# A transformer block's down projection, regrouped: two runs of 16 Strassen tiles for two of 12, its sums folded in by accumulating DMAs

## The chip, the core and the metric

The kernel runs on one core of a Trainium2 chip. The metric is the device time of one execution in microseconds (us); the runs shown are three, and one further execution was recorded with the hardware profiler.

## The reference, cut to what matters

One decoder layer on x of 512 tokens by 2048 features, all in fp32: a norm, a mixer (an mLSTM and a retention head group) and its output projection, then a SwiGLU feed-forward layer with 5632 hidden columns, and a last norm.

```python
def swiglu_ffn(h, w_gu, w_down):
    gate, up = jnp.split(h @ w_gu, 2, axis=-1)
    return (jax.nn.silu(gate) * up) @ w_down
...
        x = x + mixers[layer](rms_norm(x, mix_norms[layer]))
        x = x + swiglu_ffn(rms_norm(x, ffn_norms[layer]), *ffn_weights[layer])
    return rms_norm(x, final_norm)
```

The change lies in the last product, `@ w_down`: its 5632 input rows are 44 tiles of 128, each to be multiplied with 16 tiles of 128 output rows, for 512 tokens.

## The kernel before, in words

**Numbers.** Every fp32 operand is split into a rounded high part and the rest: ScalarE (ACT) casts the high part, VectorE (DVE) subtracts it (`split`, L80). A plain product is then three matmuls of 512 columns (`mm3`, L88 to L91). A Strassen product (`strassen`, L208 on) takes a pair of output tiles and pairs of input tiles, splits the tokens in halves of 256, and makes seven products instead of eight; in each, an input pair costs one matmul of 512 columns (L220) and one of 256 (L219 or L223). For this it needs combinations of the activations (`combinations`, L153: from each pair x seven blocks `cb`, three by the function `two` at L158 and L159, four more after the sums of L165 to L168), and of each weight: four blocks b11, b21, b12, b22 are loaded (L227), added up (L232) and split (L84, L85).

**The down projection, stage by stage.** The hidden tiles lie in DRAM (`hd`), the residual too (`resd`). 44 tiles are taken as 4 plain, 12 by Strassen, 4 plain, 12 by Strassen, 4 and 4 plain, and the last 4 in the tail, which is written apart (L963 on) because it feeds the last norm and the output. A plain stage (`plainly`) goes through eight steps q. Step q loads a pair x of hidden tiles for the Strassen stage that follows (L863; into the ring `e4` of four buffers) and makes its combinations, loads the running sum into `r` (L865) and a block of weights (L75), makes 48 matmuls, adds their two sums to `r` on DVE (L871) and stores it (L872). A Strassen stage goes through eight pairs of output tiles, and stores its results apart (L880). The block `down` loads the sums into SBUF (`res`, L900), adds the matmuls of the last plain stages (L143), the stored Strassen results (L928, L929), loads the weights of the tail (`keep`, L919), and the tail follows.

**What sets the order.** Each engine runs its instructions in one order, which a scheduler has set when the program is built, and each waits for semaphores. SP issues nearly all the DMAs, one after the other: one whose buffer isn't free holds up those behind it. Two rings matter here: `e4` (four buffers of 512 KB, for x and for the Strassen results, two for a pair of output tiles) and `r4`, which serves sums and weights alike.

## Time and profile before the change

| | |
|---|---|
| runs shown | 2264.6, 2265.9, 2263.87 us; median 2264.6 us |
| profiled execution | 2263.38 us, of which the span between its first and last instruction is 2261.3 us |
| busy: TensorE, VectorE, ScalarE, GpSimd | 99%, 87%, 52%, 1% of the span |
| from the first plain stage to the tail | 1791.25 to 2202.84 us |
| tail | 2202.84 to 2261.30 us |

The profiled execution is 1.2 us under the median. A stage of the down projection begins with the first matmul of its kind; so its length is the difference of two start times of TensorE's timeline. The busy share of an engine is a mean over the stretch that the row names.

### The profile page before, as it was taken

The page shows a single profiled execution, that of the slowest core. Times are in us where ns is not written, and L with a number is a line of the kernel's source. Part 1 is how long each engine was busy: PE and PEld are TensorE (multiplying, and loading weights), DVE is VectorE, ACT ScalarE, POOL GpSimd, SP SyncE. Part 2 cuts the span into 40 slices and gives each one's busy share as a digit, 9 for nine tenths or more (in the row PEclk, how much of TensorE's full clock was granted, in tenths as well). Part 3 has the DMA queues.
Part 4 walks back from the last instruction along what each step waited for, and adds up shares of the span by engine and source line. Part 5 has one row for each costly group of instructions (what it writes and reads, how often), then busy time and mean ns, then how long its engine had stood idle before and what let it go on. Part 6 is the DMA issues. An engine that isn't in the chain of part 4 may idle for free.

```text
span 2261.3 us, 31321 instructions
## 1 busy us (share of the span) xinstructions
PE 2246.0 (99%) x12158; PEld 1928.9 (85%) x12158; DVE 1976.1 (87%) x2441; ACT 1165.0 (52%) x1558; POOL 18.4 (1%) x33
## 2 busy tenths in 40 slices
PE   9999999999999999999999999999999999999998
PEld 7888888888887888888888888888888888888887
DVE  7898999989978876899998999999999899899686
ACT  7444454545567744555445445544544545545334
POOL 0000000000000000000000000000000000000000
PEclk9999999999999999999999999999999999999999
DMA  7444433443475424433333333333333664764772
GB/s 272 160 140 140 131 128 134 140 133 129 140 243 177 154 89 142 165 112 127 124 113 118 125 118 117 126 126 117 112 126 117 214 227 151 265 203 157 257 254 75
DMA packets 133379, 344.67 MB, mean 152 GB/s; under 512 B 12496, under 2 KB 50800, under 8 KB 133232
## 3 DMA queue, kind: packets, MB, share of 16 engines
q1 hardware_dynamic: 132656, 341.64, 45.2%
q8 instruction: 95, 1.56, 0.3%
q10 hardware_dynamic: 576, 1.05, 0.1%
q14 instruction: 52, 0.43, 0.1%
HBM read 289.15 MB, written 53.49 MB: 152 GB/s over the span
## 4 chain that ended last, share of the span: by engine, by line
PE 94%; DVE 2%; DMA 2%; issue 1%; ACT 1%; POOL 0%; SPq 0%; POOLq 0%; ACTq 0%; DVEq 0%
PE a L220 28%; PE c L220 14%; PE a L223 12%; PE b L220 7%; PE c L223 6%; PE mm L91 3%; PE mm L90 3%; PE mm L89 3%; PE b L223 3%; PE a L219 2%; PE num L651 1%; PE c L90 1%; PE c L91 1%; PE c L89 1%; PE c L219 1%
## 5 line engine op out<-in xcount | busy, mean ns | idle before, releaser
L220 PE MATMUL a<-cb,whi 128*128 128x512 f32 x2508 | 901.3, 398 | 0.0
L223 PE MATMUL a<-cb,wlo 128*128 128x256 f32 x2186 | 613.2, 281 | 0.0
L220 PEld LDWEIGHTS a<-cb,whi 128*128 128x128 f32 x2508 | 467.1, 188 | 85.2 <-issue 0.2
L85 DVE TENSOR_TENSOR wlo<-r,whi 128x1024 fp32r<-128x1024 f32 (+1 forms) x402 | 480.0, 1195 | 63.0 <-ACT whi L84 61.1
L84 ACT CAST whi<-r 128x1024 fp32r<-128x1024 f32 (+1 forms) x402 | 414.4, 1032 | 92.4 <-PE b L220 61.4
L220 PE MATMUL c<-cb,whi 128*128 128x512 f32 x1248 | 453.9, 397 | 0.2 <-ACT whi L84 0.2
L84 ACT CAST whi<-raw 128x1024 fp32r<-128x1024 f32 (+1 forms) x237 | 246.2, 1039 | 348.0 <-PE c L220 126.1
L223 PEld LDWEIGHTS a<-cb,wlo 128*128 128x128 f32 x2186 | 412.9, 189 | 14.6 <-issue 0.2
L85 DVE TENSOR_TENSOR wlo<-raw,whi 128x1024 fp32r<-128x1024 f32 (+1 forms) x237 | 285.1, 1204 | 35.4 <-ACT whi L84 34.6
L223 PE MATMUL c<-cb,wlo 128*128 128x256 f32 x1088 | 305.2, 281 | 0.0
L220 PEld LDWEIGHTS c<-cb,whi 128*128 128x128 f32 x1248 | 234.9, 188 | 42.8 <-ACT whi L84 0.6
L232 DVE TENSOR_TENSOR r<-r,r 128x1024 f32<-128x1024 f32 (+1 forms) x180 | 210.8, 1171 | 14.5 <-DMA r<-in_w_gu 11.9
L220 PE MATMUL b<-cb,whi 128*128 128x512 f32 x612 | 222.7, 398 | 0.4 <-ACT whi L84 0.4
L223 PEld LDWEIGHTS c<-cb,wlo 128*128 128x128 f32 x1088 | 205.5, 189 | 7.2
L223 PE MATMUL b<-cb,wlo 128*128 128x256 f32 x534 | 149.9, 281 | 0.8 <-DVE wlo L85 0.8
L220 PEld LDWEIGHTS b<-cb,whi 128*128 128x128 f32 x612 | 115.2, 188 | 21.6 <-ACT whi L84 0.8
L271 DVE TENSOR_TENSOR e<-e 128x512 f32<-128x512 f32 x176 | 120.7, 689 | 7.9 <-ACT e L268 5.9
L268 ACT COPY e<-a 128x512 f32<-128x512 f32 x88 | 51.8, 588 | 142.7 <-PE a L220 142.7
L256 ACT COPY e<-a 128x512 f32<-128x512 f32 x88 | 51.8, 588 | 139.3 <-PE a L220 138.1
L232 DVE TENSOR_TENSOR r<-raw,r 128x1024 f32<-128x1024 f32 (+1 forms) x88 | 103.4, 1174 | 15.5 <-DMA r<-in_w_gu 7.3
L223 PEld LDWEIGHTS b<-cb,wlo 128*128 128x128 f32 x534 | 100.9, 189 | 4.5 <-DVE wlo L85 1.1
L232 DVE TENSOR_TENSOR r<-r,raw 128x1024 f32<-128x1024 f32 (+1 forms) x84 | 98.8, 1177 | 4.1 <-DMA raw<-in_w_gu 2.6
(350 smaller groups left out, 3373.1 us busy)
## 6 DMA issues: line engine op xcount, KB each, us to landing
r<-in_w_gu SPq DMA_DIRECT2D x85, 512.0 KB, 4.2
raw<-in_w_gu SPq DMA_DIRECT2D x83, 512.0 KB, 3.2
r<-in_w_in SPq DMA_DIRECT2D x61, 512.0 KB, 4.1
raw<-in_w_in SPq DMA_DIRECT2D x59, 512.0 KB, 3.3
pd<-e SPq DMA_DIRECT2D x64, 256.0 KB, 2.3
raw<-in_w_out SPq DMA_DIRECT2D x32, 512.0 KB, 3.4
raw<-in_w_down SPq DMA_DIRECT2D x32, 512.0 KB, 4.6
r<-in_w_pairs SPq DMA_DIRECT2D x34, 384.0 KB, 4.1
```

The lines of the kernel that those rows point to most:

```text
L84: nc.scalar.copy(hi, raw)
L85: nc.vector.tensor_tensor(out=lo, in0=raw, in1=hi.bitcast(F32), op=ALU.subtract)
L89: nc.tensor.matmul(acc, wh, xh, start=first, stop=False)
L90: nc.tensor.matmul(acc, wh, xl, start=False, stop=False)
L91: nc.tensor.matmul(acc, wl, xh, start=False, stop=last)
L219: nc.tensor.matmul(*small, start=False, stop=False, skip_group_check=not first)
L220: nc.tensor.matmul(acc, wh[:, ks], cbs[k][:, c, :, :], start=(first and k == 0), stop=last, skip_group_check=not first)
L223: nc.tensor.matmul(*small, start=False, stop=False, skip_group_check=not first)
L232: nc.vector.tensor_add(t, x, y)
L256: nc.scalar.copy(two[:, 1], a)
L268: nc.scalar.copy(one[:, 0], a)
L271: nc.vector.tensor_add(x[:, :, 0, :], x[:, :, 0, :], x[:, :, 1, :])
```

## The change

The 44 tiles are taken as 4 plain, 16 by Strassen (tiles 4 to 19), 4 plain (20 to 23), 16 by Strassen (24 to 39), and 4 in the tail (40 to 43). So both Strassen stages take eight input pairs instead of six, their blocks of weights are 512 KB instead of 384 KB, and the two plain stages ahead of the tail go. A plain stage now loads no running sum: ACT copies its two sums out of PSUM (L869), and they are stored in `plain_sums` (L870). From there, and from the results of the Strassen stages in SBUF, DMAs that add to what their destination holds bring them into the residual in DRAM: those of L880 (DRAM to DRAM) and L847 (SBUF to DRAM), each 128 rows of 512, 64 in all, issued by GpSimd (POOL), which issued none before. The tail's weights are loaded at L890, its hidden tiles at L900, the residual at L915; the tail's own lines stand 22 lower than before (L962 was L984).

```diff
-        sums = [dram.tile([KT // 2, P, 2, T], F32, name="sum%d" % i) for i in range(4)]
-
-        def parts_of(g):
+
+        def add_to_residual(q, n, t):
+            nc.gpsimd.dma_start(out=resd[q][:, n, :].rearrange("p (h t) -> p h t", h=2), in_=t, accum_op=ALU.add)
+
+        plain_sums = [dram.tile([KT // 2, P, 2, T], F32, name="sum%d" % i) for i in range(2)]
+
+        def plainly(g, src, base, out):
             parts = []
             for i in range(4 * g, 4 * g + 4, 2):
                 raw, hi, lo = r4([P, 2, T]), r4([P, 2, T], F32R), r4([P, 2, T], F32R)
...
                 nc.scalar.copy(hi, raw)
                 nc.vector.tensor_tensor(out=lo, in0=raw, in1=hi.bitcast(F32), op=ALU.subtract)
                 parts += [(hi[:, e, :], lo[:, e, :]) for e in range(2)]
-            return parts
-
-        def plainly(g, src, out):
-            parts = parts_of(g)
-            _, cbs, combine = combinations(cbp, None, lambda q: None, n_pairs=6)
+            _, cbs, combine = combinations(cbp, None, lambda q: None, KT // 2)
             for q in range(KT // 2):
-                if q < 6:
-                    x = ep.tile([P, 2, T], F32, name="e4")
-                    nc.sync.dma_start(out=x, in_=hd[4 * g + 4 + q:4 * g + 11 + q:6].rearrange("j p t -> p j t"))
+                x = ep.tile([P, 2, T], F32, name="e4")
+                nc.sync.dma_start(out=x, in_=hd[base + q:base + q + 9:8].rearrange("j p t -> p j t"))
                 r = r4([P, 2, T])
-                nc.sync.dma_start(out=r, in_=src[q])
-                wh, wl = (w.rearrange("p (n k c) -> p n k c", n=2, k=4) for w in weight(w_down[g][q]))
+                wh, wl = (w.rearrange("p (n k c) -> p n k c", n=2, k=4) for w in weight(src[q]))
                 for n in range(2):
                     acc = psf.tile([P, T], F32, name="abc"[(2 * q + n) % 3])
                     for k in range(4):
                         mm3(acc, wh[:, n, k, :], wl[:, n, k, :], parts[k][0], parts[k][1], k == 0, k == 3)
-                    nc.vector.tensor_add(r[:, n, :], r[:, n, :], acc)
+                    nc.scalar.copy(r[:, n, :], acc)
                 nc.sync.dma_start(out=out[q], in_=r)
-                if q < 6:
-                    combine(q, x)
-            return cbs
-
-        def kept_sum(out):
+                combine(q, x)
+                if q > 0:
+                    combine.sums(q - 1)
+            return cbs, lambda: combine.sums(KT // 2 - 1)
+
+        def into_residual(q, plain):
             def done(one, two):
+                for i in range(q + (q > 0), min(q + 2, KT // 2)):
+                    for n in range(2):
+                        nc.gpsimd.dma_start(out=resd[i][:, n, :], in_=plain[i][:, n, :], accum_op=ALU.add)
                 for n, t in enumerate((one[:, :, 0, :], two[:, :, 0, :])):
-                    nc.sync.dma_start(out=out[:, n, :].rearrange("p (h t) -> p h t", h=2), in_=t)
+                    add_to_residual(q, n, t)
 
             return done
 
-        for i, src in enumerate((resd, sums[0])):
-            cbs = plainly(4 * i, src, sums[2 * i])
-
-            his, los = (cbp.tile([P, 3, WU], F32R, name="cb") for _ in range(2))
-            more = itertools.cycle([w for n in range(3) for w in (None, (his[:, n], los[:, n]))])
-            all_pairs([(w_pairs[i, q], kept_sum(sums[2 * i + 1][q])) for q in range(KT // 2)], cbs, ep, psf, {})
-            more = itertools.repeat(None)
-        parts = parts_of(8)
+        kept, parts = [], []
+
+        def keep(i, tile_of):
+            raw = wp.tile([P, WU], F32, name="raw")
+            nc.sync.dma_start(out=raw, in_=w_last[i])
+            kept.append(split(raw, tile_of(), tile_of()))
+
+        for i in range(2):
+            cbs, last_sums = plainly(5 * i, w_down[5 * i], 4 + 20 * i, plain_sums[i])
+            all_pairs([(w_pairs[i, q], into_residual(q, plain_sums[i])) for q in range(KT // 2)], cbs, ep, psf, {}, last_sums)
+
+        for i in range(FT - 4, FT, 2):
+            raw = wp.tile([P, WU], F32, name="raw")
+            raw = raw.rearrange("p (j t) -> p j t", j=2)
+            nc.sync.dma_start(out=raw, in_=hd[i:i + 2].rearrange("j p t -> p j t"))
+            for e in range(2):
+                both, src = r4([P, 2, 2, HT], F32R), raw[:, e, :].rearrange("p (x t) -> p x t", x=2)
+                nc.scalar.copy(both[:, :, 0, :], src)
+                nc.vector.tensor_tensor(out=both[:, :, 1, :], in0=src, in1=both[:, :, 0, :].bitcast(F32), op=ALU.subtract)
+                parts.append(both)
+        for i in range(3):
+            keep(i, lambda: r4([P, WU], F32R))
 
     with ExitStack() as down:
         dp = down.enter_context(tc.tile_pool(name="dp", bufs=2, reuse_waits="tile"))
         ep = down.enter_context(tc.tile_pool(name="ep2", bufs=4, side="right", reuse_waits="tile"))
         psd = down.enter_context(tc.tile_pool(name="psd", bufs=1, space=bass.MemoryType.PSUM, reuse_waits="tile"))
-        accs.append(psd)
         for q in range(KT // 2):
             pairs[q] = dp.tile([P, 2, T], F32, name="res", bufs=8)
-            nc.sync.dma_start(out=pairs[q], in_=sums[2][q])
-
-        def group(g):
-            raw = dp.tile([P, 4, T], F32, name="hr", bufs=1)
-            both = dp.tile([P, 4, 2, T], F32R, name="hs")
-            nc.sync.dma_start(out=raw, in_=hd[4 * g:4 * g + 4].rearrange("j p t -> p j t"))
-            if g < FT // 4 - 1:
-                src, hi, lo = raw, both[:, :, 0, :], both[:, :, 1, :]
-            else:
-                both = both.rearrange("p j x (h t) -> p j x h t", h=2)
-                src, hi, lo = raw.rearrange("p j (x t) -> p j x t", x=2), both[:, :, :, 0, :], both[:, :, :, 1, :]
-            nc.scalar.copy(hi, src)
-            nc.vector.tensor_tensor(out=lo, in0=src, in1=hi.bitcast(F32), op=ALU.subtract)
-            return [(hi[:, e], lo[:, e]) for e in range(4)] if g < FT // 4 - 1 else both
-
-        kept = []
-
-        def keep(q):
-            raw = wp.tile([P, WU], F32, name="raw")
-            nc.sync.dma_start(out=raw, in_=w_last[q])
-            if q < 5:
-                hi, lo = r4([P, WU], F32R), r4([P, WU], F32R)
-            else:
-                hi, lo = (dp.tile([P, WU], F32R, name="kept", bufs=6) for _ in range(2))
-            kept.append(split(raw, hi, lo))
-
-        def add_sum(i, q):
-            x = ep.tile([P, 2, T], F32, name="e4")
-            nc.sync.dma_start(out=x, in_=sums[i][q])
-            nc.vector.tensor_add(pairs[q], pairs[q], x)
-
-        def last_sum(q):
-            keep(q)
-            add_sum(3, q)
-
-        nxt = group(9)
-        residual_gemm(w_down[8], parts, lambda q: add_sum(1, q))
-        parts, nxt = nxt, group(10)
-        residual_gemm(w_down[9], parts, last_sum)
-        parts = nxt
+            nc.sync.dma_start(out=pairs[q], in_=resd[q])
+            if 1 <= q < 6:
+                keep(q + 2, lambda: dp.tile([P, WU], F32R, name="kept", bufs=10))
 
 
 
...
                 r = res(q + 8 * n)[:, 0:HT]
                 for k in range(4):
                     wh, wl = (w[:, k % 2, i * P:(i + 1) * P] for w in kept[2 * blk + k // 2])
-                    x = parts[:, k, 0]
+                    x = parts[k][:, 0]
                     small = (acc[:, 0, :], wl, x[:, 0])
                     if k == 3:
                         nc.tensor.matmul(*small, start=False, stop=False)
...
                 acc = psd.tile([P, T], F32, name="mm", bufs=4)
                 for k in range(4):
                     wh, wl = (w[:, k % 2, :] for w in kept[2 * blk + k // 2])
-                    xh, xl = parts[:, k, 1, 0, cols], parts[:, k, 1, 1, cols]
+                    xh, xl = (parts[k][:, 1, i, cols] for i in range(2))
                     mm3(acc, xh, xl, wh, wl, k == 0, k == 3)
                 bs = slice(blk % 2 * T, (blk % 2 + 1) * T)
                 u, g = turned[c][blk // 2][:, bs], g_row[blk // 2][:, bs]
...
     def paired(w):
-        v = w.reshape(2, 6, P, 2, 8, P)
-        return c(v.transpose(4, 3, 0, 2, 1, 5)).reshape(8, 2, 2, P, 6 * P)
+        v = w.reshape(2, 8, P, 2, 8, P)
+        return c(v.transpose(4, 3, 0, 2, 1, 5)).reshape(8, 2, 2, P, WU)
...
-        w_pairs=np.stack([paired(w_down[k * P:(k + 12) * P]) for k in (4, 20)]),
+        w_pairs=np.stack([paired(w_down[k * P:(k + 16) * P]) for k in (4, 24)]),
```

On DVE, the middle of the second plain stage before. `e4_17650`, `e4_17699` and `e4_17748` are the pairs x of its steps 2, 3 and 4; L159 is the split of a pair's first three combinations, L165 to L168 are its four sums, L168 the last reader of x.

```order
L159 TENSOR_TENSOR cb_17738<-e4_17699,cb_17738 128x3x256
L871 TENSOR_TENSOR r4_17603<-r4_17603,a_17625 128x512
L165 TENSOR_TENSOR r4_17741<-e4_17650 128x256
L167 TENSOR_TENSOR r4_17741<-e4_17650 128x256
L166 TENSOR_TENSOR r4_17741<-r4_17741,e4_17650 128x256
L85 TENSOR_TENSOR wlo_17755<-raw_17752,whi_17754 128x1024
L871 TENSOR_TENSOR r4_17652<-r4_17652,b_17660 128x512
L168 TENSOR_TENSOR r4_17741<-e4_17650,r4_17741 128x256
L159 TENSOR_TENSOR cb_17787<-e4_17748,cb_17787 128x3x256
L165 TENSOR_TENSOR r4_17790<-e4_17699 128x256
```

And now, where `e4_17908`, `e4_17956`, `e4_18052` and `e4_18100` are the pairs of steps 1, 2, 4 and 5:

```order
L159 TENSOR_TENSOR cb_18090<-e4_18052,cb_18090 128x3x256
L168 TENSOR_TENSOR r4_17997<-e4_17908,r4_17997 128x256
L85 TENSOR_TENSOR wlo_18106<-raw_18103,whi_18105 128x1024
L159 TENSOR_TENSOR cb_17946<-r4_17997,cb_17946 128x4x256
L165 TENSOR_TENSOR r4_18045<-e4_17956 128x256
L167 TENSOR_TENSOR r4_18045<-e4_17956 128x256
L166 TENSOR_TENSOR r4_18045<-r4_18045,e4_17956 128x256
L159 TENSOR_TENSOR cb_18138<-e4_18100,cb_18138 128x3x256
L168 TENSOR_TENSOR r4_18045<-e4_17956,r4_18045 128x256
L85 TENSOR_TENSOR wlo_18154<-raw_18151,whi_18153 128x1024
L159 TENSOR_TENSOR cb_17994<-r4_18045,cb_17994 128x4x256
```

Before, the last sum of step 2 stands ahead of the split of step 4. Now the last sum of step 1 stands behind the split of step 4, that of step 2 behind the split of step 5, and so on to step 7; the additions of L871 have left DVE.

On SP, the end of the second plain stage before; `r4_17971` is the block b21 for the second pair of output tiles of the Strassen stage, `r4_17975` its b22.

```order
L872 DMA sum2_16067<-r4_17799 128x1024
L227 DMA raw_17969<-in_w_pairs 128x768
L227 DMA r4_17971<-in_w_pairs 128x768
L227 DMA r4_17973<-in_w_pairs 128x768
L872 DMA sum2_16067<-r4_17853 128x1024
L227 DMA r4_17975<-in_w_pairs 128x768
L227 DMA raw_18199<-in_w_pairs 128x768
L872 DMA sum2_16067<-r4_17890 128x1024
```

And now, where `r4_18248` and `r4_18250` are b12 and b22 of the first pair of output tiles, `r4_18303` is b21 of the second:

```order
L870 DMA sum1_16066<-r4_18102 128x1024
L870 DMA sum1_16066<-r4_18150 128x1024
L227 DMA r4_18248<-in_w_pairs 128x1024
L227 DMA r4_18250<-in_w_pairs 128x1024
L870 DMA sum1_16066<-r4_18198 128x1024
L227 DMA r4_18303<-in_w_pairs 128x1024
L227 DMA r4_18305<-in_w_pairs 128x1024
L227 DMA r4_18307<-in_w_pairs 128x1024
L227 DMA raw_18595<-in_w_pairs 128x1024
```

The block b21 of the second pair stood ahead of the stores of the last two sums; now it stands behind the store of the last one.

On SP, the last loads ahead of the tail before:

```order
L75 DMA raw<-in_w_down 128x1024
L928 DMA e_19712<-sum_16068 128x1024
L919 DMA raw<-in_w_last 128x1024
L949 DMA grow<-in_g_last 128x1024 x2
L997 DMA outT<-o 128x2x256 x7
```

And now:

```order
L900 DMA raw<-hd 128x2x512 x2
L890 DMA raw<-in_w_last 128x1024 x5
L927 DMA grow<-in_g_last 128x1024 x2
L890 DMA raw<-in_w_last 128x1024
L915 DMA res<-resd 128x1024 x5
L890 DMA raw<-in_w_last 128x1024
L915 DMA res<-resd 128x1024
L890 DMA raw<-in_w_last 128x1024
L915 DMA res<-resd 128x1024 x2
L975 DMA outT<-o 128x2x256 x7
```

The residual, which came into `res` at the start of `down` before, is now loaded last, behind the loads of `grow` and of the tail's weights.

## Rows read from the trace of the kernel before

**Rows 1.** The page: busy us, share of the span and instructions

```profile
PE 2246.0 (99%) x12158; PEld 1928.9 (85%) x12158; DVE 1976.1 (87%) x2441; ACT 1165.0 (52%) x1558; POOL 18.4 (1%) x33
```

**Rows 2.** Windows: w_gu, five stages (two plain groups in the fifth), tail

```profile
core 0: us, PE busy (x) PEld busy (x) DVE busy (x) ACT busy (x) POOL busy (x), PEclk, DMA share, GB/s
1600.00:1700.00 100.00, 100.00 (x570) 86.99 (x569) 91.44 (x97) 49.95 (x61) 0.00 (x0) 1.00 0.37 123
1791.25:1834.79 43.54, 43.54 (x193) 36.04 (x192) 40.80 (x59) 19.58 (x22) 0.00 (x0) 1.00 0.86 300
1834.79:1952.60 117.81, 117.81 (x673) 102.78 (x672) 105.10 (x134) 64.11 (x90) 0.00 (x0) 1.00 0.53 175
1952.60:1996.14 43.54, 43.54 (x194) 36.04 (x192) 38.97 (x58) 18.68 (x21) 0.00 (x0) 1.00 0.91 300
1996.14:2113.95 117.81, 117.81 (x674) 102.78 (x672) 104.07 (x129) 63.26 (x88) 0.00 (x0) 1.00 0.48 151
2113.95:2202.84 88.89, 87.66 (x385) 71.85 (x384) 67.14 (x71) 26.37 (x24) 0.00 (x0) 1.00 0.83 296
2202.84:2261.30 58.46, 50.28 (x275) 42.96 (x273) 37.00 (x79) 24.62 (x52) 1.80 (x3) 0.96 0.21 72
```

**Rows 3.** Waits of PE from 1791 us on: total, times, longest

```profile
PE mm L91 <- DVE wlo L85: 1.1, 1, 1.1
```

**Rows 4.** Timeline of PE, w_gu: first matmuls of two successive pairs (start, us)

```profile
1754.59 0.40 PE L220 MATMUL b<-cb,whi 128*128 128x512 f32 x1
...
1774.33 0.40 PE L220 MATMUL b<-cb,whi 128*128 128x512 f32 x1
```

**Rows 5.** DMA in the first plain stage: KB each, median us to landing

```profile
q1 hardware_dynamic: 4550, 13.04, 85.8%
...
sum<-r SPq DMA_DIRECT2D x7, 512.0 KB, 3.7
e<-hd SPq DMA_DIRECT2D x4, 512.0 KB, 4.7
raw<-in_w_down SPq DMA_DIRECT2D x4, 512.0 KB, 6.0
```

**Rows 6.** DMA in the Strassen stage behind it

```profile
sum<-e SPq DMA_DIRECT2D x15, 256.0 KB, 2.3
...
e<-hd SPq DMA_DIRECT2D x2, 512.0 KB, 4.0
```

**Rows 7.** Groups by form, ACT, same Strassen stage: busy us, mean ns

```profile
L251 ACT COPY e<-a 128x512 f32<-128x512 f32 x8 | 4.7, 588 | 6.1 <-PE a L220 6.1
...
L84 ACT CAST whi<-raw 128x1024 fp32r<-128x1024 f32 x3 | 3.2, 1054 | 3.4 <-PE c L220 2.7 <-PE b L220 0.8
...
L158 ACT CAST cb<-e 128x768 fp32r<-128x768 f32 x2 | 1.6, 832 | 0.0
```

**Rows 8.** Groups by form, DVE, first plain stage

```profile
L85 DVE TENSOR_TENSOR wlo<-raw,whi 128x1024 fp32r<-128x1024 f32 x7 | 8.6, 1223 | 0.0
...
L159 DVE TENSOR_TENSOR cb<-e,cb 128x768 fp32r<-128x768 f32 x6 | 5.7, 955 | 0.1
...
L168 DVE TENSOR_TENSOR r<-e,r 128x256 f32<-128x256 f32 x4 | 1.7, 424 | 0.0
```

**Rows 9.** Two of eight `res` loads in a row: issue, us to landing

```profile
2115.95 0.42 SPq L900 DMA_DIRECT2D res<-sum  x1
DMA to landing us min/median/max: 5.6/5.6/5.6
...
2117.86 0.96 SPq L900 DMA_DIRECT2D res<-sum  x1
DMA to landing us min/median/max: 9.4/9.4/9.4
```

**Rows 10.** SP's issue of b21 for the second pair, first plain stage; its landing

```profile
1826.52 0.41 SPq L227 DMA_DIRECT2D r<-in_w_pairs  x1
...
DMA to landing us min/median/max: 5.1/5.1/5.1
```

**Rows 11.** The page, DMA issues: a load where DMA is a third busy

```profile
raw<-in_w_gu SPq DMA_DIRECT2D x83, 512.0 KB, 3.2
```

**Rows 12.** Timeline of PE in the tail: first transposes of the residual

```profile
2208.49 1.04 PE L984 MATMUL tp<-ident,res 128*128 128x128 f32 x8
```

## The prediction

> **What bounds the kernel now.** I read the page first: TensorE (PE) is busy 99% of the span, VectorE 87% [rows 1]; so PE sets the time unless it is made to wait. The windows by stage come next, because the share over the whole span hides stages with other limits [rows 2]: the two plain stages take 43.54 us each, the two Strassen stages 117.81 each, the two plain groups ahead of the tail 88.89. PE is busy all of the first four; DVE is busy too, for 38.97 to 40.80 of 43.54 us in the plain stages. The list of what PE waited for holds one wait of 1.1 us from the first plain stage to the end [rows 3]. So whoever takes matmuls away gets their time, as long as the two engines that prepare operands, and the DMAs behind them, keep up. That is where this change is decided: DMA is at a share of 0.86 and 0.91 in the plain stages, against 0.53 and 0.48 in the Strassen ones [rows 2].
>
> **What goes and comes on PE.** An input tile costs 43.54/4 = 10.89 us plain. A run of eight input pairs by Strassen is what the w_gu stage does all along, and two successive pairs of output tiles start there at 1754.59 and 1774.33 us, 19.74 us apart [rows 4]. Eight pairs of output tiles make 157.92 us for 16 input tiles, 9.87 us a tile.
> - Removed: 2 x 117.81 + 88.89 = 324.51 us.
> - Added: 2 x 157.92 = 315.84 us.
> - The two plain stages with 43.54 us stay, and the tail does the same matmuls in its 58.46 us.
> So PE's gain is 324.51 − 315.84 = 8.67 us, if it waits for nothing new. The 88.89 us hold the 1.1 us wait, which goes with its stage.
>
> **DVE and ACT.** In the Strassen stages DVE has per pair of output tiles eleven operations on blocks of weights (seven splits, four sums), now 128x1024 at 1.22 us [rows 8] and so some 13.5 us, and about 3.4 us on results: 17 of 19.74 us. In the w_gu stage it is busy 91.44% with more on its hands and PE never waits [rows 2]; no cost. In the plain stages DVE loses 16 additions and gets the combinations of two more pairs, about as much; ACT gets 16 copies of 0.588 us [rows 7], 9.4 us in a stage in which it is busy 19.58 of 43.54 us. No cost by themselves. POOL issues 64 DMAs and has been idle in all of this [rows 2].
>
> **The second plain stage: a chain of loads.** Here the order matters. The pairs x go through a ring of four buffers. Pair 4 can be loaded when pair 0 was last read, pair 5 after pair 1, and so on; and now the last read of pair 1 stands on DVE behind the split of pair 4, that of pair 2 behind the split of pair 5. So each step is one round trip: load, cast on ACT 0.83 us [rows 7], split 0.95 and last sum 0.42 on DVE [rows 8]. The load took 4.0 us in a Strassen stage [rows 6] and 4.7 in a plain one [rows 5], where 3.2 is the median of a load with DMA a third busy [rows 11]. With 3.2 the trip is 5.4 us, just one step of PE (43.54/8 = 5.44); with 4.7 it is 6.9. I take 4.4, as the accumulating DMAs run at the same time: 6.6 us, 1.16 us over a step, four times over (pairs 4 to 7): 4.6 us of lag; bounds 0 and 5.9. Before, only pairs 4 and 5 had to be reloaded and the order left them two steps. The lag first uses up what DVE is ahead; I put 3.0 us of it on PE.
>
> At the end of that stage b21 of the second pair of output tiles is issued behind the last sum's store. That store follows the last matmul by an ACT copy (0.588) and some hand-over, about 1.0 us, and b21's issue by another 0.4, as an issue takes [rows 9, 10]; the store ahead of it in the queue takes about 1.4 us (two `res` loads landed at 2121.55 and 2127.26 with four landings from one to the other [rows 9]), a load by itself 3.2 [rows 11]. So it lands about 6.0 us after the last plain matmul. PE needs its split after three products of 19.74/7 = 2.82 us, at 8.46, less the cast of 1.05 [rows 7]: 7.4. With an accumulating DMA of 2 x 256 KB in between it lands at 7.4, and the split's DVE part (1.22 us) then costs about 1 us. Before, b21 was issued 8.27 us ahead of the stage's end and took 5.1 [rows 2, 10]. Together 4.0 us at the second start; bounds 0 and 6.9.
>
> At the first start the order still leaves the pairs more room (only one of them chained so), and b21 stands ahead of the last store: 1.0 us, bounds 0 and 4.6.
>
> **The tail.** The residual's loads come last now. By the order the first `res` load waits for the last pair's first product block, the others for its end; transposes need them from 2208.49 − 2202.84 = 5.65 us behind the tail's start [rows 2, 12], a lone load takes 3.2. I put 0.1 us on it.
>
> **The accumulating DMAs.** No trace shows one. Below, one can't be cheaper than nothing; the nearest row is the plain store of 256 KB with 2.3 us to landing [rows 6], which is where I put it (one copy's time on the engines, k = 1); above, several copies. In a plain stage SP moves about 13 MB, 25 copies of 512 KB [rows 5], at 1.4 us 35 us of 43.54. Sixteen accumulates of 256 KB are 8 such copies, 11.2k us. But the last two steps' (2.8k) may run into the Strassen stage. So 8.5 us are free for 8.4k: with k = 1 there is room, with much more there is none.
>
> The Trainium skill speaks against the change here: "Collectives: The Full Stack", section "The bandwidth ceiling: the fold count and why AG ≠ RS ≠ AR", says that a DMA which adds reads two sources for every write, and measured a reduce at 1/1.93 of a copy's rate. No run here shows it. By that rule k is about 2, and the time is that of the third case below.
>
> **The sum.** 8.67 − 4.0 − 1.0 − 0.1 = 3.6 us off the profiled 2263.38 us, 2259.8; it is 1.2 us below the median of 2264.6, so against the runs shown 2261.0 us.
>
> **The rivals.**
> 1. *The loads keep up.* If accumulates leave SP's loads alone (landing in 3.2 to 3.6 us), the round trip fits in a step and b21 lands before 7.4: 8.67 less some 0.7 for the starts, 2256.6 us. For it: a load's median is 3.2 us with DMA at 0.37 [rows 2, 11]. Against it: plain stages have 4.7 and 6.0 us already [rows 5].
> 2. *Part of it is lost, the forecast*, 2261.0 us; its own range 2257.5 to 2265.5.
> 3. *Slower: the DMA engines become the bound of the plain stages.* With k = 2 the engines' work by the end of a plain stage is 35 + 8.4 x 2 = 51.8 us, 8.3 over; it falls on the chained pairs and on b21, and PE waits for it at both starts: 16.6 − 8.67 = 7.9 us slower, 2272.5 us. It turns slower where 2 x (35 + 8.4k − 43.54) is over 8.67: k above 1.53. For it: the share of 0.86 and 0.91 [rows 2], the lack of any row of such a DMA, and that each reads and writes DRAM. Against it: a queue that is only busy isn't late, and the engines had 8.5 us to spare in that count.
> The Trainium skill, "DMA: Bandwidth & Descriptors", section "SWDGE vs HWDGE vs iDMA", has each DMA engine take turns between the queue of POOL's DMAs and that of SP's. No run here shows it; by it rival 1 is the less likely, as accumulates are not put behind SP's loads.
> 4. *The tail waits.* If the `res` load for the second block stands behind two `grow` loads, a load of weights and the first `res` (4 x 1.4 + 1.4 + 3.2 = 10.2 us), PE stands still for 10.2 − 5.65 = 4.6 us, on top of the forecast: 2265.6 us. For it: the order of those rows on SP. Against it: `grow` waits for a product that is some 5 us ahead of the stage's end, so most of that queue has run by then.
>
> **How the numbers follow.** What can be told from no change is about 0.2%, 4.5 us: faster is under 2260.1, slower over 2269.1. The forecast has 0.40 (0.12 of it under 2260.1, 0.28 within), the loads that keep up 0.26 (0.25 faster, 0.01 within), the DMA bound 0.25 (0.22 slower, 0.03 within), the waiting tail 0.09 (0.06 within, 0.03 slower). That makes 0.37 faster, 0.38 within, 0.25 slower. The range goes from 2256.0, where all costs but the starts' smallest vanish, to 2272.5, the third case's own time; about 0.2 is left out, most of it above.
>
> **What the profile would show.** The steps on PE: Strassen stages of about 158 us and plain ones of 43.5. The chain: in the second plain stage DVE's splits of pairs 4 to 7 (L159) each end a wait for `e<-hd`, over 5.44 us apart, and PE waits at the start of the second Strassen stage for b21's split, first of all in `b` at L220. A landing of the accumulating DMAs of 2.3 to 3.5 us would speak for k = 1, over 5 us for the DMA bound; then both starts would show waits of some 8 us. The tail: a wait of PE ahead of the transposes, released by a `res` load. I am wrong if PE waits in the midst of a Strassen or a plain stage, for a buffer which an accumulating DMA holds, or if the starts cost nothing and the time is still above 2260.

## The result

The changed kernel takes 2284.46 us (median of four runs, 2276.99 to 2289.52) against 2265.2 us for the kernel before in the same comparison: ratio 1.0084, interval 1.0071 to 1.0096. It is 19 us slower; I had forecast 2261.0 us, and even the slow rival at 2272.5 us is too low. The profiled execution is the slowest of the four, 2289.52 us with a span of 2287.7 us, 5 us above the median; so the losses read from it are somewhat larger than a usual execution has.

The windows by stage of the changed kernel (first and second plain and Strassen stage, tail), which answer to [rows 2]:

```profile
core 0: us, PE busy (x) PEld busy (x) DVE busy (x) ACT busy (x) POOL busy (x), PEclk, DMA share, GB/s
1794.00:1837.55 43.55, 43.55 (x194) 36.04 (x193) 31.57 (x47) 24.66 (x33) 8.53 (x10) 1.00 0.92 279
1837.55:2007.01 169.46, 161.56 (x897) 138.98 (x896) 139.37 (x144) 82.52 (x98) 22.66 (x21) 0.98 0.61 157
2007.01:2056.10 49.09, 45.90 (x193) 36.83 (x191) 28.29 (x41) 23.55 (x32) 9.79 (x12) 0.97 0.91 247
2056.10:2229.31 173.21, 163.49 (x896) 140.95 (x897) 140.99 (x149) 82.19 (x99) 22.66 (x21) 0.96 0.61 161
2229.31:2287.70 58.39, 50.26 (x275) 42.96 (x273) 40.27 (x83) 29.20 (x58) 3.30 (x5) 0.96 0.50 172
```

The first plain stage and the tail are as before. The Strassen stages take 169.46 and 173.21 us instead of the 157.92 that their matmuls need, the second plain stage 49.09 instead of 43.54: 11.54 + 15.29 + 5.55 = 32.4 us lost, against the 8.67 that the new grouping saves. That is 23.7 us from the first plain stage to the tail; the rest of the 26.4 us between the two spans lies ahead of it (see run b_again below).

All of the loss sits where a Strassen stage begins, and in the last steps of the second plain stage. What PE waited for from the first plain stage to the tail (total, times, longest), which answers to [rows 3]:

```profile
PE b L220 <- ACT whi L84: 13.5, 4, 6.4
PE b L223 <- DVE wlo L85: 2.4, 4, 0.8
PE a L220 <- ACT r L869: 2.3, 2, 1.5
PE c L89 <- ACT whi L84: 0.9, 1, 0.9
PE a L223 <- DVE wlo L85: 0.8, 1, 0.8
PE c L91 <- DVE wlo L85: 0.8, 1, 0.8
```

These make 20.7 us; by the windows PE stands still for 20.8 us (7.90, 3.19 and 9.72 of the three stages). The other 11.6 us are matmuls that took longer, and most of that is TensorE's clock. In four stretches, all behind or within waits, the granted clock is at the lower of its two levels, 1.2 instead of 2.4 GHz. Three of them lie in these windows, the fourth in the second plain stage; in the rest of the stages the clock is at 1.00:

```profile
1850.00:1870.00 20.00, 15.19 (x73) 12.62 (x72) 14.43 (x14) 9.05 (x11) 1.65 (x2) 0.83 0.91 264
...
2056.10:2070.00 13.90, 11.09 (x44) 9.10 (x45) 12.41 (x20) 7.01 (x9) 3.30 (x4) 0.75 0.99 243
2070.00:2090.00 20.00, 13.10 (x63) 10.76 (x62) 11.91 (x11) 7.54 (x9) 1.66 (x2) 0.83 0.79 240
```

By these shares 20 x 0.17 + 13.9 x 0.25 + 20 x 0.17 + 49.09 x 0.03 = 11.7 us of clock are missing. But part of them falls into the waits themselves, where a low clock costs nothing, as in the longest one:

```profile
2070.92:2077.36 6.44, 0.00 (x1) 0.00 (x0) 0.02 (x1) 1.04 (x1) 1.66 (x2) 0.83 1.05 360
```

That is 1.1 us here (6.44 x 0.17), and some 2.5 us over all waits by my estimate from such rows. So the clock explains about 9 of the 11.6 us; the remaining 2 or so should lie in the matmuls next to a wait, which have no neighbour to overlap with (an estimate by difference; in the stream a matmul listed with 0.40 us and one with 0.28 take a step of 0.35). A timeline of PE at the longest wait shows the step from one matmul to the next; the pair of a 512 and a 256 columns takes 0.35 us at full clock (2070.06 to 2070.41) and 0.65 us after the wait (2079.00 to 2079.65), the lower of the two levels, 1.2 GHz:

```profile
2070.06 0.40 PE L220 MATMUL a<-cb,whi 128*128 128x512 f32 x1
...
2070.41 0.28 PE L219 MATMUL a<-cb,wlo 128*128 128x256 f32 x1
...
2077.36 0.80 PE L220 MATMUL b<-cb,whi 128*128 128x512 f32 x1 [6.44 <-ACT whi L84]
...
2079.00 0.63 PE L220 MATMUL b<-cb,whi 128*128 128x512 f32 x1
...
2079.65 0.63 PE L220 MATMUL b<-cb,whi 128*128 128x512 f32 x1
```

That wait can be followed back. It ends with ACT's cast of b21 of the second pair, the place that the prediction named. On SP's timeline b21 is issued behind the store of the last sum, 9.43 us after the second Strassen stage's start, and lands 10.7 us later; on ACT's, the copy of that last sum (L869) stands behind a cast that waits for DVE's last sum of a pair x (L168):

```profile
2065.11 0.33 SPq L870 DMA_DIRECT2D sum<-r  x1
2065.53 0.44 SPq L227 DMA_DIRECT2D r<-in_w_pairs  x1
...
DMA to landing us min/median/max: 10.7/10.7/10.7
```

```profile
2063.55 1.05 ACT L158 CAST cb<-r 128x1024 fp32r<-128x1024 f32 x1 [2.27 <-DVE r L168]
2064.51 0.58 ACT L869 COPY r<-a 128x512 f32<-128x512 f32 x1
...
2076.27 1.04 ACT L84 CAST whi<-r 128x1024 fp32r<-128x1024 f32 x1 [8.47 <-DMA r<-in_w_pairs]
```

And DVE is late because of the chain of loads. SP's issues of the pairs x 4 to 7 in the second plain stage:

```profile
2020.98 0.37 SPq L862 DMA_DIRECT2D e<-hd  x1
...
2027.29 0.37 SPq L862 DMA_DIRECT2D e<-hd  x1
...
2035.76 0.37 SPq L862 DMA_DIRECT2D e<-hd  x1
...
2046.53 0.37 SPq L862 DMA_DIRECT2D e<-hd  x1
```

6.3, 8.5 and 10.8 us apart, where a step of PE is 5.44. The chain also begins late. Four loads of x wait until the adds of the last Strassen results have landed, because these hold the four buffers; before the change the stores of those results held them for much less. SP's waits (total, times, longest) at the second plain stage, before and now:

```profile
SPq L863 <- DMA sum<-e: 2.2, 4, 0.8
```

```profile
SPq L862 <- DVE r L168: 19.4, 4, 9.2
SPq L862 <- DMA resd<-e: 12.5, 4, 6.6
```

The DMAs of that stage (KB each, median us to landing), against [rows 5]:

```profile
q1 hardware_dynamic: 3366, 9.46, 55.7%
q0 software_dynamic: 1703, 2.64, 35.0%
...
e<-hd SPq DMA_DIRECT2D x6, 512.0 KB, 5.9
sum<-r SPq DMA_DIRECT2D x6, 512.0 KB, 6.8
resd<-sum POOLq DMA_DIRECT2D x10, 256.0 KB, 7.7
```

POOL's queue takes 35.0% of the sixteen engines' time for 2.64 MB, SP's 55.7% for 9.46 MB: 6.5 against 2.9 us of all engines per MB (of 49.09 us).

### The profile page after: what moved, and what is told of

It is laid out like the page before. It is cut to its first block, busy times and chain, and to the rows that moved or that the text cites. A ratio compares the mean times of both kernels' runs of the same rounds, so it can differ in the third digit from the quotient of the medians.

```text
span 2287.7 us, 31383 instructions
## 1 busy us (share of the span) xinstructions
PE 2251.9 (98%) x12222; PEld 1933.1 (85%) x12222; DVE 1960.3 (86%) x2369; ACT 1188.6 (52%) x1582; POOL 83.5 (4%) x97
## 3 DMA queue, kind: packets, MB, share of 16 engines
q0 software_dynamic: 13312, 16.78, 4.9%
## 4 chain that ended last, share of the span: by engine, by line
PE 82%; issue 7%; DMA 4%; DVE 4%; ACT 1%; POOL 1%; SPq 0%; POOLq 0%; ACTq 0%; DVEq 0%
PE a L220 26%; PE c L220 13%; PE a L223 11%; PE b L220 6%; PE c L223 6%; PE b L223 3%; PE mm L91 2%; PE mm L90 2%; DMA e<-hd 2%; PE mm L89 2%; PE a L219 2%; DMA ld<-pd 1%; DVE z L629 1%; PE c L219 1%; PE num L651 1%
## 5 line engine op out<-in xcount | busy, mean ns | idle before, releaser
L220 PE MATMUL a<-cb,whi 128*128 128x512 f32 x2816 | 1011.8, 398 | 2.3 <-ACT r L869 2.3
L223 PE MATMUL a<-cb,wlo 128*128 128x256 f32 x2464 | 691.6, 281 | 0.8 <-DVE wlo L85 0.8
L85 DVE TENSOR_TENSOR wlo<-r,whi 128x1024 fp32r<-128x1024 f32 x444 | 541.2, 1220 | 88.1 <-ACT whi L84 86.5
L220 PEld LDWEIGHTS a<-cb,whi 128*128 128x128 f32 x2816 | 524.6, 188 | 99.7 <-ACT r L869 3.0
L84 ACT CAST whi<-r 128x1024 fp32r<-128x1024 f32 x444 | 467.0, 1053 | 124.1 <-PE b L220 75.9
L220 PE MATMUL c<-cb,whi 128*128 128x512 f32 x1408 | 512.0, 398 | 0.2 <-ACT whi L84 0.2
L84 ACT CAST whi<-raw 128x1024 fp32r<-128x1024 f32 x235 | 246.9, 1051 | 320.2 <-PE c L220 142.0
L85 DVE TENSOR_TENSOR wlo<-raw,whi 128x1024 fp32r<-128x1024 f32 x235 | 286.5, 1220 | 26.3 <-ACT whi L84 25.6
L220 PEld LDWEIGHTS c<-cb,whi 128*128 128x128 f32 x1408 | 265.0, 188 | 48.7 <-ACT whi L84 0.6
L220 PE MATMUL b<-cb,whi 128*128 128x512 f32 x704 | 262.0, 405 | 13.9 <-ACT whi L84 13.9
L232 DVE TENSOR_TENSOR r<-r,r 128x1024 f32<-128x1024 f32 x180 | 219.6, 1220 | 20.0 <-DMA r<-in_w_gu 16.8
L220 PEld LDWEIGHTS b<-cb,whi 128*128 128x128 f32 x704 | 135.3, 192 | 40.5 <-ACT whi L84 15.5
L232 DVE TENSOR_TENSOR r<-raw,r 128x1024 f32<-128x1024 f32 x88 | 107.6, 1223 | 23.0 <-DMA r<-in_w_pairs 8.3
L232 DVE TENSOR_TENSOR r<-r,raw 128x1024 f32<-128x1024 f32 x84 | 102.5, 1220 | 7.1 <-DMA raw<-in_w_pairs 3.3
```

Of the source, the lines that this page charges most:

```text
L84: nc.scalar.copy(hi, raw)
L85: nc.vector.tensor_tensor(out=lo, in0=raw, in1=hi.bitcast(F32), op=ALU.subtract)
L220: nc.tensor.matmul(acc, wh[:, ks], cbs[k][:, c, :, :], start=(first and k == 0), stop=last, skip_group_check=not first)
L223: nc.tensor.matmul(*small, start=False, stop=False, skip_group_check=not first)
L232: nc.vector.tensor_add(t, x, y)
```

## The experiments

Loss below is what the three late stages take over 157.92, 43.54 and 157.92 us in a run's profile; in the changed kernel it is 11.5, 5.5 and 15.3 us. A loss is that of one execution: the profile of the changed kernel lies 5.1 us above its median, that of e2 3.7, e4 3.1, e8 2.5 and e3 1.9, the others within 0.7. So the text gives differences of medians beside differences of losses.

**Without the adds of the plain sums (e1_no_plain_adds).** They never reach the residual.

```diff
-                for i in range(q + (q > 0), min(q + 2, KT // 2)):
-                    for n in range(2):
-                        nc.gpsimd.dma_start(out=resd[i][:, n, :], in_=plain[i][:, n, :], accum_op=ALU.add)
```

> The 32 accumulating DMAs of L880 (plain sums, DRAM to DRAM) are left out, so the sums of the two plain stages never reach the residual; the 32 of L847 stay. Theory A (the L880 DMAs take the DMA engines in the plain stages, and SP's loads come late for it): the second plain stage goes back to 43.5 us, both Strassen stages to 158 to 161 us, time 2256 to 2260 us. Theory C (the chain of x loads through four buffers, and b21 behind the last store, are late by themselves): the second plain stage and the start of the second Strassen stage keep half of their loss or more, 2268 us or more. Theory D (the adds of the Strassen results, L847, hold the buffers that x needs): nearly all of the loss stays, 2275 us or more.

2264.64 us, ratio 1.000 (0.9991 to 1.0009). Loss 0.5, 0 and 7.0 us:

```profile
1995.33:2038.87 43.54, 43.54 (x193) 36.04 (x192) 29.64 (x44) 23.58 (x32) 1.50 (x2) 1.00 0.78 242
2038.87:2203.82 164.95, 161.03 (x898) 138.37 (x896) 140.94 (x147) 82.07 (x99) 17.82 (x15) 0.99 0.56 153
```

So these 32 DMAs carry 24.9 of the 32.4 us (19.8 us by the medians). But the time is neither the 2256 to 2260 us that theory A alone wants nor the 2268 us of theory C: the second Strassen stage starts late without them too, and x 4 to 7 are still issued 6.64, 6.44 and 6.31 us apart:

```profile
2009.77 0.37 SPq L862 DMA_DIRECT2D e<-hd  x1
...
2016.41 0.37 SPq L862 DMA_DIRECT2D e<-hd  x1
...
2022.85 0.37 SPq L862 DMA_DIRECT2D e<-hd  x1
...
2029.16 0.37 SPq L862 DMA_DIRECT2D e<-hd  x1
```

**Copies in the adds' place (e2_copies).** All 64 DMAs of POOL copy, those of L847 too; no sum reaches the residual; `spare` is DRAM that nothing reads.

```diff
-nc.gpsimd.dma_start(out=resd[i][:, n, :], in_=plain[i][:, n, :], accum_op=ALU.add)
+nc.gpsimd.dma_start(out=spare[plain_sums.index(plain)][i][:, n, :], in_=plain[i][:, n, :])
...
```

> All 64 DMAs of POOL stay at their places and with their bytes, but copy into spare DRAM instead of adding, so no sum reaches the residual. Theory A1 (adding is what is dear: a second read for each write): an L880 DMA lands in 3 to 4 us instead of 5 to 11, and the time is 2258 to 2266 us, as my forecast had it with one copy's cost. Theory A2 (POOL's queue, or a transfer from DRAM to DRAM, is dear whether it adds or not): landings stay over 5 us and the time over 2272 us.

2273.89 us, ratio 1.0043 (1.0029 to 1.0056). By its time, over 2272 us, and by the copies' landings, over 5 us, theory A2 holds; the engines' time further down speaks for A1 as well. Loss 6.2, 4.8 and 10.0 us, 21.0 in all. Adding itself thus makes 11.4 of the 32.4 us (10.6 by the medians), and the transfers cost 13.5 us more than e1 (9.3 by the medians) although they only copy. They do so with room on the engines, at DMA shares of 0.85 and 0.77 in the plain stages. The first plain stage, and the landings of the 32 copies of plain sums in the whole run:

```profile
1793.01:1836.53 43.52, 43.52 (x193) 36.04 (x192) 32.12 (x48) 24.55 (x33) 5.41 (x10) 1.00 0.85 291
```

```profile
spare<-sum POOLq DMA_DIRECT2D x32, 256.0 KB, 5.7
```

SP's loads of x land after a median of 6.5 and 5.1 us in the two plain stages, against 5.3 and 4.3 us in e1, and PE waits 4.6 us for ACT's copy of a plain sum (`PE a L220 <- ACT r L870`). Whether the second queue, the way from DRAM to DRAM or the moment at which the copies fall makes them dear, no run separates.

The queue rows of the two pages (packets, MB, share of 16 engines of the span), of the changed kernel and of e2:

```profile
q0 software_dynamic: 13312, 16.78, 4.9%
```

```profile
q0 software_dynamic: 5120, 16.78, 2.2%
```

2287.7 x 0.049 / 16.78 = 6.68 us of all engines per MB for adds, 2275.8 x 0.022 / 16.78 = 2.98 for copies: k is 2.24, for the same bytes in 2.6 times the packets. This is a mean of two kinds, which e1 (results alone, out of SBUF) and e8 below (plain sums alone, DRAM to DRAM) show apart:

```profile
q0 software_dynamic: 8704, 8.39, 2.7%
```

```profile
q0 software_dynamic: 4608, 8.39, 2.2%
```

2262.2 x 0.027 / 8.39 = 7.28 us per MB for the results' adds, 2.4 times a copy; 2282.2 x 0.022 / 8.39 = 5.98 for those of the plain sums, in about half the packets: 2.0 times. (The Trainium skill, "Collectives: The Full Stack", section "The bandwidth ceiling: the fold count and why AG ≠ RS ≠ AR", has a reduce at 1/1.93 of a copy's rate because it reads two sources. For the plain sums' adds the rows agree, 1.9 to 2.1 by the rounding of the shares; those out of SBUF are dearer, 2.3 to 2.5, and there the measurement decides.)

**The adds of a plain sum behind those of the results (e3_after_results).**

```diff
+                for n in range(2):
+                    nc.gpsimd.dma_start(out=resd[q][:, n, :], in_=plain[q][:, n, :], accum_op=ALU.add)
```

(after the adds of the Strassen result of the same q, in place of the loop that e1 leaves out).

> All adds are made; those of a plain sum (L880) are issued behind the adds of the Strassen result into the same rows, and so wait for them: they move out of the plain stage, into the Strassen stage, two per pair of output tiles, where DMA is half busy. Theory A: plain stages 43.5 us, Strassen stages 158 to 162 us, time 2256 to 2261 us, faster than before by 0.2 to 0.4%. Theories C and D: the second plain stage stays over 46 us and the time over 2270 us.

2272.25 us, ratio 1.0031 (1.0018 to 1.0043). It takes off 12 us but misses its expectation. Loss 3.5, 0.3 and 12.8 us. The plain stages are clean, but now there are waits in the midst of a Strassen stage (1.8 us `PE a L220 <- DVE e L264` at 2169.67 us). Followed back, this one ends with a block of weights that landed 8.5 us after SP issued it at 2158.0 us, while POOL's adds were moving. And the adds of the first stage's last results still hold x 2 and 3 of the second plain stage (SP waits 5.3 us for them).

**Without any adds (e4_none)**, and **without reloading x 4 to 7 (e6_no_reload)**. The first leaves out all adds, the second those of the plain sums, and makes the combinations for x 4 to 7 from x 0 to 3.

```diff
+                x = xs[q - 4] if q > 3 else ep.tile([P, 2, T], F32, name="e4")
+                xs.append(x)
+                if q < 4:
                     nc.sync.dma_start(out=x, ...
```

> All 64 accumulating DMAs are left out; neither the plain sums nor the Strassen results reach the residual. What is left is the work on TensorE, VectorE and ScalarE and SP's DMAs. Theory E (in the second plain stage the pairs x 2 and 3 wait until the adds of the last Strassen results have landed, which hold their buffers; DVE, nearly full, never catches up that late start): with no such adds the second Strassen stage takes 158 to 159 us and the time is 2256 to 2258 us. Theory C (the round trip of each x through four buffers is longer than a step by itself): the second Strassen stage stays over 161 us, 2260 us or more. If 2 us are still lost ahead of the first plain stage, they have nothing to do with POOL's DMAs.

> As e1 (no adds of plain sums), and the pairs x 4 to 7 of both plain stages are not loaded: the combinations are made from x 0 to 3 again, so the Strassen stages work with wrong inputs. The chain of loads is gone, and four of SP's loads per stage with it; x 2 and 3 of the second plain stage still wait for the adds of the last Strassen results. Theory C: the second Strassen stage falls from 165 us to 158 to 160 us, time some 2258 us. Theory E: it stays at 163 to 165 us, time 2262 to 2265 us.

e4: 2259.38 us, ratio 0.9974 (0.9964 to 0.9983); loss 0.9, 0 and 3.6 us, so its second Strassen stage, 161.56 us, is where theory C has it, and its time lies between the two. e6: 2259.65 us, ratio 0.9975 (0.9965 to 0.9984); loss 0.3, 0 and 3.0 us, a second Strassen stage of 160.91 us, also between the two and nearer to theory C. Against e1, taking the chain away gives back 4.0 us of 7.0 in the second Strassen stage, as theory C has it, though not all; taking the results' adds away gives 3.4. So both delay the same start: the adds make the chain begin late (theory E), and the chain keeps it late. Which of them has the larger share in the kernel as it was changed, these two runs don't settle.

**Without the adds of the results (e8_no_result_adds).** They never reach the residual; the plain sums' adds stay.

> The 32 adds of the Strassen results (L847) are left out, those of the plain sums stay; the results never reach the residual. Theory A (the adds of L880 make the loss): first Strassen stage still 168 to 170 us, second 168 to 173 us, time 2278 us or more. Theory D (results that hold the buffers of x make the loss): the second plain stage 43.5 us, the second Strassen stage under 162 us, time under 2270 us.

2281.56 us, ratio 1.0074 (1.0060 to 1.0088); loss 10.2, 0.1 and 14.7 us. Theory A holds and theory D falls, except for one thing: the 5.5 us of the second plain stage are gone. There it took both kinds of adds.

**Added straight from SBUF (v10_direct).** Every sum in its place.

```diff
-                nc.sync.dma_start(out=out[q], in_=r)
+                nc.gpsimd.dma_start(out=resd[q], in_=r, accum_op=ALU.add)
```

> Every sum is in its place, but a plain sum is added to the residual straight from SBUF by one DMA of 512 KB, with no store into plain_sums: in a plain stage SP moves 8 copies of 512 KB less, and no DMA goes from DRAM to DRAM; the bytes added are the same. Theory A1 (adding is dear, some 2.2 times a copy's engine time): 17 + 8 x 2.2 = 35 copies of 1.4 us, 48 us of engine time for 43.5 us: a part of the loss stays, Strassen stages 161 to 165 us, time 2263 to 2272 us. Theory A2 (the transfer from DRAM to DRAM is what is dear): Strassen stages 158 to 161 us but for the chain of x, time 2258 to 2264 us.

2271.17 us, ratio 1.0031 (1.0020 to 1.0042); Strassen stages of 165.34 us both, loss 7.4, 0 and 7.4 us, and 0.9 in the first plain stage. With 8 copies less per stage for SP and nothing from DRAM to DRAM about half of the loss stays, as theory A1 has it (its stages are 0.3 us longer than that). An add out of SBUF thus costs no less: the page has 4.9% of the span for 16.78 MB, 6.63 us per MB. The first Strassen stage shows something else:

```profile
1836.60:2001.94 165.34, 159.30 (x896) 137.32 (x897) 140.51 (x147) 82.33 (x98) 19.40 (x17) 1.00 0.58 150
```

PE stands still for 6.0 us in it, in several waits, and the granted clock stays at 1.00. So not every wait brings the clock down.

**A mend (v16_chain_sums), and its chain shortened (v17a).** v16 adds only the Strassen results by DMA, into the plain sums in DRAM; each plain stage loads the running sum and adds to it on DVE, as before the change. v17a puts two of the eight x into the other ring.

```diff
                 r = r4([P, 2, T])
+                nc.sync.dma_start(out=r, in_=prev[q])
...
-                    nc.scalar.copy(r[:, n, :], acc)
+                    nc.vector.tensor_add(r[:, n, :], r[:, n, :], acc)
...
-                x = ep.tile([P, 2, T], F32, name="e4")
+                x = r4([P, 2, T]) if q in (5, 7) else ep.tile([P, 2, T], F32, name="e4")
```

> A mend with every sum in its place: the plain stages load the running sum and add to it on DVE as before the change, and the adds of the Strassen results go into that stage's plain sums in DRAM, which the next plain stage (or the tail) loads. So the DMAs of L880 go, SP loads 8 sums of 512 KB per plain stage more, DVE adds 16 times per plain stage. Theory A (L880 in the plain stage is what made the change slow): plain stages 43.6 us, Strassen stages 158 to 161 us, time 2256 to 2261 us. Theory F (SP's queue in the plain stage is full already, and any added load makes b21 late): the Strassen stages stay over 163 us and the time over 2264 us.

> The mend v16, with the pairs x 5 and 7 of a plain stage in buffers of the other ring (r4), so that the chain of loads through the four buffers has two links instead of four. Theory C (the chain is what still delays the second Strassen stage's start): both Strassen stages 158 to 159 us, 1 us less than v16, time 2258 to 2260 us. Rival: the r4 ring, which holds sums and weights, becomes the next wait: Strassen stages over 160 us, time over 2262 us.

v16: 2260.84 us, ratio 0.9980 (0.9971 to 0.9988), Strassen stages of 159.63 and 159.34 us, as theory A has it. v17a: 2257.95 us, ratio 0.9971 (0.9959 to 0.9982), the lowest median of all, though its interval overlaps with those of v16, e4 and e6. Its stages, of which the last is 0.1 us longer than theory C has it:

```profile
1793.40:1836.92 43.52, 43.52 (x193) 36.04 (x192) 41.85 (x63) 19.85 (x23) 0.00 (x0) 1.00 0.89 313
1836.92:1995.11 158.19, 158.05 (x898) 137.23 (x897) 136.64 (x144) 78.88 (x94) 17.63 (x15) 1.00 0.57 159
1995.11:2038.63 43.52, 43.52 (x193) 36.03 (x192) 40.78 (x60) 20.29 (x22) 1.87 (x2) 1.00 0.94 308
2038.63:2197.74 159.11, 158.30 (x897) 137.17 (x896) 136.72 (x139) 77.84 (x93) 17.74 (x15) 1.00 0.55 154
```

DVE is at 41.85 of 43.52 us in the plain stage and DMA at 0.89 and 0.94, and yet PE waits once, 0.7 us, and the clock stays up. SP moves 8 copies more per plain stage than in the changed kernel; so a full queue of SP's alone does not do it (theory F falls), and neither does a high DMA share: the changed kernel has 0.92 and 0.91 in its plain stages. These two kernels also have no copies of sums on ACT, so what they gain is not the adds' alone.

**The kernel before once more (b_again).**

> The kernel before, once more, for its profile. In every kernel since, the first plain stage began at 1793.0 to 1794.6 us instead of 1791.25 us, also with no DMA of POOL at all. If that is scatter between executions (the opening, before TensorE's clock is up), this profile shows a first plain stage at 1792 to 1794 us too; if the change causes it, at 1791.2 to 1791.6 us.

2265.53 us. Its first plain stage begins at 1793.17 us, its stages are those of [rows 2] within 0.4 us. So 1.9 us of the opening are scatter between two executions of the same kernel. TensorE's first matmuls of 512 columns show what it is, one from the first profile and one from this:

```profile
6.74 0.42 PE L347 MATMUL a<-cb,whi 128*128 128x512 f32 x1
```

```profile
9.17 0.63 PE L347 MATMUL b<-cb,whi 128*128 128x512 f32 x1
```

A length of 0.63 us is that of the lower clock, as above. In the first profile such matmuls end at about 6.7 us, here they go on to about 10.2 us; 3.5 us more at half speed are about 1.7 us. The profile of the changed kernel has them until 9.15 us at least, so most of its 2.75 us ahead of the first plain stage are of this kind and no effect of the change.

## Why the prediction was wrong, by its own steps

- *PE's gain, 8.67 us.* Right. v17a keeps it but for some 1.5 us, and PE's busy time per stage without waits is as worked out.
- *The second plain stage's chain.* Right in place and mechanism: the trip was put at 6.6 us, and e1 measures 6.3 to 6.6. Its price at the second start was 4.0 us; e1, without the plain sums' adds, shows 7.0, of which 3.9 us are waits and about 1.6 the clock (164.95 x 0.01). Taking the chain away gives back 4.0 (e6). But 3.4 go as well when the results' adds are taken away (e4): that they hold the buffers of x, and so make the chain begin late, was in no term.
- *The first start, 1.0 us.* 0.5 us in e1; 11.5 with the adds.
- *The accumulating DMAs, k = 1 and room for it.* This is the step that failed, in its size and in its overlap. The size: the prediction took "the plain store of 256 KB with 2.3 us to landing" for the nearest row. Measured, an add takes 2.24 times the engines' time of a copy (2.0 times for those of the plain sums), and a plain sum's adds landed 7.7 us after issue in the second plain stage. That is worth 10.6 us, the medians of the changed kernel against e2. The overlap: "with k = 1 there is room". e2 is that case, and it is 12.9 us slower than the forecast; e1, without these transfers, is 3.6 us slower. So 9.3 us come with transfers that cost the engines no more than a copy and were put at nothing. How much of that is the queue and how much the way from DRAM to DRAM stays open.
- *The third case.* It had the DMA bound, k = 2, and waits at both starts, 16.6 us; the waits are 20.7. The place and the price of an add were right in it. But that the sum comes near is in part luck. It carried SP's 13 MB and 35 us over from [rows 5], a stage that still loaded running sums; without the adds SP moves 10.95 and 9.96 MB in 73.6% and 68.0% of 43.54 us, 32.0 and 29.6 us (e1). With these the same sum gives 5.3 + 2.9 = 8.1 us.
- *What the waits cost besides.* The third case stopped there: 16.6 − 8.67 = 7.9 us slower. It left out that PE's matmuls take longer around such waits. That is 11.6 us more, most of it the clock, a term which the prediction did not have at all, and without which 20.8 us of waits give 12.1 us instead of the measured 23.7 in the profiled execution. The tail's PEclk of 0.96 before the change [rows 2] was no hint of it: there the clock is low behind PE's last matmul (0.52 from 2256.00 to 2261.30 us, where PE is busy for 0.00 us).
- *What was asked of the profile.* "PE waits at the start of the second Strassen stage for b21's split, first of all in `b` at L220": it does, and at the first start as well; only the first 1.5 us at the second start are a wait for ACT's copy of a sum. "over 5 us for the DMA bound; then both starts would show waits of some 8 us": landings of 7.7 us, waits of 8 and 10.
- *The tail.* Right: 58.39 us, no wait for `res`.
- *DVE and ACT, no cost by themselves.* Right for DVE: it is busy for 31.57 and 28.29 us in the plain stages, in part because it waits for x there. ACT's copies are cheap, but they put PE's sums into a queue behind casts that wait for DVE, and so carry the chain's lag to SP's stores and to b21; the prediction had costed the copies by their duration alone.

## What to carry to other kernels

A DMA that adds is not a store: here it took the engines twice as long as a copy, or more. And room on the DMA engines is not yet time to spare: mere copies in POOL's queue cost 9.3 us (by the medians) beside SP's loads at DMA shares of 0.85 and 0.77, while a kernel with nearly all its plain-stage transfers in SP's queue ran at 0.89 and 0.94 with one wait. So try the transfers as copies first, before pricing the addition. A wait of TensorE can cost more than its length; in this kernel 20.8 us of waits cost 32.4, most of the rest through the clock. And before a ring of few buffers is made to feed a longer loop, add up one round trip, from load to last reader, compare it with a step, and ask which DMA sets the buffers free at its start.

## What the runs showed of the hardware

An accumulating DMA took 6.68 us of all sixteen engines per MB against 2.98 for the same bytes copied from the same queue, and 2.6 times the packets. The plain sums' adds, DRAM to DRAM, took 5.98 (e8), the results' adds, out of SBUF and in nearly twice the packets, 7.28 (e1); plain sums added straight from SBUF leave the mean at 6.63 (v10). After some waits TensorE ran at the lower of its two clocks (0.65 us instead of 0.35 for a 512 and a 256 column matmul), which makes up about 9 of the 11.6 us that the changed kernel loses beyond its 20.8 us of waits. After others it did not: v10's first Strassen stage has 6.0 us of waits at a granted clock of 1.00. At the start of an execution the lower clock lasted to about 6.7 us in one profile of the kernel before and to about 10.2 us in the other, which is most of the 1.9 us between them.
